# Router products and sums of squares computed as four 32-column strips of TensorE

## The chip, the cores and the metric

One core of a Trainium2 chip runs the whole kernel. The metric is device time of one execution in microseconds (us). The kernel before has a median of 809.95 us over three runs, which lie between 808.85 and 810.82 us. The profile is of one further execution, taken by the hardware profiler.

## The reference, cut to what matters

One decoder layer on 1024 tokens of width 1024, in float32: a norm with a modulation, two parallel branches (causal attention with 4 heads, and a recurrent branch of width 512), their projection added to the residual, then a router and 32 experts of which each token uses two.

```python
h = rms_norm(x, norm1_g) * (1.0 + scale1) + shift1
proj = h @ w_in
q_lat, kv_lat, k_rope, x_lru, g_lru = split(proj)
attn = mla_attention(q_lat, kv_lat, k_rope, ...)
lru = rg_lru_branch(x_lru, g_lru, ...)
mixed = concat([rms_norm(attn, attn_out_norm), rms_norm(lru, lru_out_norm)])
x = x + gate1 * (mixed @ w_out)
h2 = rms_norm(x, norm2_g) * (1.0 + scale2) + shift2

g_prob = softmax(t @ w_rg + b_rg)           # 4 groups; t is h2 as rows
e_logits = (t @ w_re + b_re)                # 32 experts, 8 in each group
# the best group, in it the two best experts, their weights g_p * e_p
# each expert on its tokens: (silu(xb @ w_gate[e]) * (xb @ w_up[e])) @ w_down[e]
x = x + gate2 * y
```

The change touches two things in it: the mean of the squares of `lru` over its 512 channels, for each token (inside the norm of the recurrent branch), and the 4 + 32 logits of each token.

## The kernel before, in words

The tokens are eight tiles of 128. The program goes through these stages: input projection with the recurrent branch (20 to 236 us of the profile), the projection of the recurrent branch by the lower half of `w_out` (`l_pass`, 236 to 300, merged with the preparation of the next attention heads), attention (to about 445), the projection of the attention output with the second norm, the router and the token tables (`w_steps`, mostly 445 to 515), and the experts (515 to the end), whose weights are streamed from HBM by SP in loads `ew` of 512 KB. Some of these loads are issued early, at points named by `ahead`, as far as buffers are free; at most four are in flight. SP works off its queue in order, so a store that waits holds back the weight loads behind it.

The order of instructions on each engine is not that of the code: a scheduler simulates the program as it is built and rewrites each engine's order. Any changed instruction can therefore move others. Banks of PSUM (matmul results) are handed out by tag from rings (`OPT["ph"]`): `pL` from a ring of three banks, `pr` from a ring of one, `pc2` from a ring of two that `ptq`, `ptk` and `ptk2` share.

The places that the change and the prediction touch:

- `norms` (L1055 to L1060) computes, for given tiles, the sum of squares over channels. `sqL` holds squares with channels on partitions and the 1024 tokens along the row, already added over the four channel blocks on POOL (L660). For each tile, L1059 loads 128 tokens of `sqL` as weights and multiplies by a column of ones: one column of output for each tile, with tokens on partitions. `rsq` (L197 to L213) turns it into the reciprocal root on DVE, in twelve small dependent steps, as `ivL`.
- `l_pass` (from L1062) needs `ivL` when it evicts the first product `pL` (DVE, L1082); a product is twelve matmuls of 512 columns (L225 to L227, three for each f32 product, on parts split into high and low).
- `x1_t` (L1250) transposes one token tile of the new residual (`pth`, L1257) and copies it on ACT to two halves `x1T` (L1258).
- `router(g)` (L1260 to L1268) serves a pair of tiles: with 128 tokens as weights and the 40 columns of `wrg` (4 group logits, 4 fillers, 32 expert logits) as the moving operand it accumulates eight products for each tile in `pr`. Each f32 product shows as two records in the trace.
- `route(g)` (from L1273) scales the logits by `ivx` (the second norm) and adds the bias on DVE (L1278), then finds groups, experts and weights in a chain of some thirty small DVE steps that ends in `mb` (L1311) and `rec`.
- `places(g)` (from L1319) turns `mb` into positions in the token table: PE `ppos`, DVE `scr`, `slot`, `ohs`, `rhs` (L1331 to L1342), PE `ptab` (L1345), DVE `tb` (L1350). Its `macc` carries counts from pair to pair.
- `w_steps` calls these in turn for each pair while the next pair is projected; for the last pair the router stands behind the last projection, and the table, the gathers of tokens and the first expert follow from it. `h2_rows` scales a tile by `ivx` on ACT (L1242) and stores it through SP (L1247).

Of the kernel before, what the change touches and what calls it, by code (L numbers as in the profile page):

```python
# [20 lines left out]
D = 1024  # L21
S = 1024
NT = 8
# [77 lines left out]
for _n, _w in GRP:  # L101
# [20 lines left out]
def drain(g):  # L122
    for _ in g:
        pass
# [14 lines left out]
def layer(ctx, tc, A, out, dbg=None, stop=None):  # L139
# [57 lines left out]
    def rsq(o, ss, mul, eps, shape):  # L197
        x = smc.tile(shape, F32, name="rs_x")
        V.tensor_scalar(x, ss, mul, eps, op0=OP.mult, op1=OP.add)
        yield  # L200
        i = smc.tile(shape, I32, name="rs_i")
        V.tensor_scalar(i, x.bitcast(I32), 1, None, op0=OP.logical_shift_right)
        yield
        y = smc.tile(shape, F32, name="rs_y")
        V.tensor_scalar(y.bitcast(I32), i, -1, 0x5F3759DF, op0=OP.mult, op1=OP.add)
        yield
        t = smc.tile(shape, F32, name="rs_t")
        for it in range(3):
            V.tensor_mul(t, y, y)
            yield  # L210
            V.scalar_tensor_tensor(t, t, -0.5, x, op0=OP.mult, op1=OP.mult)
            yield
            V.scalar_tensor_tensor(o if it == 2 else y, t, 1.5, y, op0=OP.add, op1=OP.mult)  # L213
            yield
# [840 lines left out]
    def norms(iv, sq, ts):  # L1055
        n = len(ts)
        pc = bank("pc2")
        for t in ts:
            T.matmul(pc[:, t:t + 1], sq[:, t * 128:(t + 1) * 128], ones_c, start=True, stop=True)  # L1059
        drain(rsq(iv[:, ts[0]:ts[0] + n], pc[:, ts[0]:ts[0] + n], 1.0 / 512, EPS, [128, n]))  # L1060

    def l_pass():  # L1062
        mod_row("g1", 2)
# [196 lines left out]
    def router(g, parts=((0, 0), (0, 1), (1, 0), (1, 1))):  # L1260
        if "pr" not in St[g]:
            St[g]["pr"] = bank("pr")
        pr = St[g]["pr"]
        for a, h in parts:
            xT = St[2 * g + a]["x1T"]
            for k in range(4 * h, 4 * h + 4):
                T.matmul(pr[:, a * 40:a * 40 + 40], xT[h][:, (k % 4) * 128:(k % 4) * 128 + 128], wrg[:, k],
                         start=(k == 0), stop=(k == 7))  # L1268

    def two(w, name, dt=F32):  # L1270
        return sm.tile([128, 2, w], dt, name=name, bufs=2)

    def route(g):  # L1273
        pr = St[g].pop("pr")
        ts = slice(2 * g, 2 * g + 2)
        L = two(40, "L")
        for a in range(2):
            V.scalar_tensor_tensor(L[:, a], pr[:, a * 40:a * 40 + 40], ivx[:, 2 * g + a:2 * g + a + 1], brow,  # L1278
                                   op0=OP.mult, op1=OP.add)
        g8, gi, gex, gp = two(8, "g8"), two(8, "gi", U32), two(4, "gex"), two(1, "gp")  # L1280
        for a in range(2):
            V.max(g8[:, a], L[:, a, :8])
        ng = two(1, "ng")
        V.tensor_scalar(ng, g8[:, :, 0:1], -1.0, None, op0=OP.mult)
        for a in range(2):
            V.max_index(gi[:, a], g8[:, a], L[:, a, :8])
            SC.activation(gex[:, a], L[:, a, :4], AF.Exp, bias=ng[:, a], accum_out=gp[:, a])
        gf = two(1, "gf")
        V.tensor_copy(gf, gi[:, :, 0:1])
        oh = two(4, "oh")  # L1290
        V.tensor_tensor(oh, iota[:, None, :4].to_broadcast([128, 2, 4]), gf.to_broadcast([128, 2, 4]), op=OP.is_equal)
        sel = two(32, "sel").rearrange("p a (g e) -> p a g e", g=4)
        V.tensor_mul(sel, L[:, :, 8:].rearrange("p a (g e) -> p a g e", g=4), oh[:, :, :, None].to_broadcast([128, 2, 4, 8]))
        el = two(8, "el")
        V.tensor_reduce(el, sel.rearrange("p a g e -> p a e g"), op=OP.add, axis=AX.X)
        V.reciprocal(gp, gp)
        e8, ei = two(8, "e8"), two(8, "ei", U32)
        for a in range(2):
            V.max(e8[:, a], el[:, a])
        d = two(1, "d")  # L1300
        V.tensor_sub(d, e8[:, :, 1:2], e8[:, :, 0:1])
        SC.activation(d, d, AF.Exp)
        for a in range(2):
            V.max_index(ei[:, a], e8[:, a], el[:, a])
        ef = two(2, "ef")
        V.tensor_copy(ef, ei[:, :, 0:2])
        V.scalar_tensor_tensor(ef, gf.to_broadcast([128, 2, 2]), 8.0, ef, op0=OP.mult, op1=OP.add)
        V.tensor_tensor(M[:, ts], iota[:, None, None, :32].to_broadcast([128, 2, 2, 32]),
                        ef[:, :, :, None].to_broadcast([128, 2, 2, 32]), op=OP.is_equal)
        mb = sm.tile([128, 2, 32], BF, name="mb", bufs=2)  # L1310
        V.tensor_add(mb, M[:, ts, 0], M[:, ts, 1])  # L1311
        w1 = two(1, "w1")
        V.tensor_scalar(w1, d, 1.0, None, op0=OP.add)
        V.reciprocal(w1, w1)
        V.tensor_mul(rec[:, ts, 0, 1:2], w1, gp)
        V.tensor_mul(rec[:, ts, 1, 1:2], rec[:, ts, 0, 1:2], d)
        St[g]["mb"] = mb
# [38 lines left out]
    def w_steps():  # L1356
        for t in range(OPT["xa"]):
            load_x1(t)
        for g in range(4):
            while g not in fin:  # L1360
                yield False
            t = 2 * g
            load_x1(t + OPT["xa"])
            load_x1(t + 1 + OPT["xa"])
            drain(w_mm(t, 0))
            if g:
                x1_t(t - 1)
                router(g - 1)
                norm2([t - 2, t - 1])
            ahead(4 * g)  # L1370
            yield True
            drain(w_mm(t, 1))
            if g:
                route(g - 1)
            x1_t(t)
            ahead(4 * g + 1)
            yield True
            drain(w_mm(t + 1, 0))
            if 0 < g < 3:
                places(g - 1)  # L1380
            ahead(4 * g + 2)
            yield True
            drain(w_mm(t + 1, 1))
            if g:
                h2_rows(t - 2)
                h2_rows(t - 1)
            ahead(4 * g + 3)
            yield True
        mod_row("g2", 5)
        ahead(16)  # L1390
        norm2([6])
        x1_t(7, (0,))
        router(3, ((0, 0), (0, 1)))
        x1_t(7, (1,))
        router(3, ((1, 0), (1, 1)))
        places(2)
        norm2([7])
        route(3)
        h2_rows(6)
        h2_rows(7)  # L1400
        ahead(17)
        places(3)
# [372 lines left out]
```

## Time and profile before

| | |
|---|---|
| median of three runs | 809.95 us (808.85 to 810.82) |
| profiled execution | 816.49 us |
| its span, first to last instruction | 814.6 us |
| mean granted clock of TensorE | 0.971 |
| PE busy | 728.1 us, 89% of the span |
| PE weight loads busy | 471.2 us, 58% (beside PE) |
| DVE, ACT, POOL busy | 447.2 us (55%), 317.0 us (39%), 157.6 us (19%) |
| moved by DMA | 180.47 MB, 222 GB/s over the span |

The profiled execution took 1.9 us more than its span, and 6.5 us more than the median. A share of busy time is an average over stages with different limits: PE is the busy engine until about 500 us, the DMA engines are the busy ones behind it. A matmul's end in the trace is modelled, so what one costs is read from the distance of two starts, not from its length. The rows further down are read in that way.

### The profile page before, as it was taken

How to read it: one execution, taken by the hardware profiler on the slowest of the kernel's cores; microseconds unless marked ns; L12 is line 12 of the kernel's file. 1: busy time of each engine (PE TensorE's matmuls, PEld its weight loads, DVE VectorE, ACT ScalarE, POOL GpSimd, SP SyncE). 2: the span in 40 equal slices, each digit the busy share in tenths (PEclk: the TensorE clock that was granted, in tenths of full speed). 3: DMA queues.
4: the chain of work that ended last, by engine and by line, in shares of the span. 5: the costliest groups of instructions: out<-in, count | busy, mean ns of one | idle time of the engine just before them, and what ended most of it. 6: DMA issues, size and time to landing. Idle time of an engine off the chain costs nothing. (4 is left out here: it accounts for less than half of the span.)

```text
span 814.6 us, 12260 instructions
## 1 busy us (share of the span) xinstructions
PE 728.1 (89%) x4257; PEld 471.2 (58%) x4257; DVE 447.2 (55%) x1334; ACT 317.0 (39%) x715; POOL 157.6 (19%) x150
## 2 busy tenths in 40 slices
PE   3899999989988989899999997699979899999874
PEld 1477776548877878788888886333333343332321
DVE  4597386868777469797884667344334222213210
ACT  3455456666354157667664434121201211102200
POOL 1121012103665102031311000212112112212010
PEclk9989999999999999999999998699989999999998
DMA  9952437681317403020154789999999999999994
GB/s 311 372 151 84 143 108 236 210 280 58 109 44 259 168 39 104 1 79 1 54 173 144 259 311 343 346 316 349 313 373 330 329 335 336 369 347 354 304 320 102
DMA packets 70976, 180.47 MB, mean 222 GB/s; under 512 B 8960, under 2 KB 22528, under 8 KB 70912
## 3 DMA queue, kind: packets, MB, share of 16 engines
q1 hardware_dynamic: 63328, 158.50, 55.1%
q0 software_dynamic: 7104, 21.00, 9.5%
q8 instruction: 34, 0.56, 0.3%
q10 hardware_dynamic: 480, 0.16, 0.2%
q14 instruction: 30, 0.25, 0.1%
HBM read 160.61 MB, written 22.95 MB: 225 GB/s over the span
## 5 line engine op out<-in xcount | busy, mean ns | idle before, releaser
L1649 PE MATMUL pgu<-ew,xeT 128*32 128x512 f32 (+1 forms) x928 | 163.4, 613 | 8.1 <-DMA ew<-in_w_e 7.3
L1649 PEld LDWEIGHTS pgu<-ew,xeT 128*32 128x32 f32 (+1 forms) x928 | 48.3, 121 | 99.4 <-issue 79.0
L1660 PE MATMUL py<-ew,hT 128*32 128x512 f32 (+1 forms) x464 | 75.1, 597 | 5.8 <-ACT hT L1634 5.8
L225 PE MATMUL pp<-hTh,winh 128*128 128x512 f32 x176 | 69.2, 406 | 5.8 <-DVE hTh L188 3.0
L226 PE MATMUL pp<-hTl,winh 128*128 128x512 f32 x176 | 71.1, 404 | 0.0
L227 PE MATMUL pp<-hTh,winl 128*128 128x512 f32 x176 | 70.4, 401 | 0.0
L1663 DVE TENSOR_TENSOR y<-py,m_g 128x512 f32<-128x512 f32 (+1 forms) x40 | 27.5, 691 | 69.3 <-PE py L1660 64.3
L1623 ACT ACTIVATE sg<-pgu 128x256 f32<-128x256 f32 (+1 forms) x20 | 7.7, 387 | 142.9 <-PE pgu L1649 135.8
L1660 PEld LDWEIGHTS py<-ew,hT 128*32 128x32 f32 (+1 forms) x464 | 23.5, 120 | 48.3 <-issue 35.7
L1616 DVE TENSOR_SCALAR xeT<-pxe,gc,mc 128x128 f32<-128x128 f32 x80 | 27.4, 404 | 33.0 <-PE pxe L1610 33.0
L225 PEld LDWEIGHTS pp<-hTh,winh 128*128 128x128 f32 x176 | 34.0, 194 | 16.3 <-DVE hTh L188 4.0
L1665 POOL DMA_INDIRECT out<-y,pki x13 | 20.7, 1589 | 111.2 <-DVE y L1663 87.7
L1625 DVE SCALAR_TENSOR_TENSOR hid<-sg,pkw,pgu 128x256 f32<-128x256 f32 (+1 forms) x13 | 6.2, 479 | 63.4 <-ACT sg L1623 60.9
L1634 ACT ACTIVATE hT<-pht 128x256 f32<-128x256 f32 (+1 forms) x20 | 7.6, 380 | 85.1 <-PE pht L1632 65.4
L1614 ACT ACTIVATE xeT<-pxe,mc,gc 128x128 f32<-128x128 f32 x80 | 30.0, 461 | 24.9 <-PE pxe L1610 24.9
L226 PEld LDWEIGHTS pp<-hTl,winh 128*128 128x128 f32 x176 | 33.9, 193 | 9.9 <-issue 2.1
L227 PEld LDWEIGHTS pp<-hTh,winl 128*128 128x128 f32 x176 | 34.1, 194 | 8.6 <-issue 1.7
L949 ACT ACTIVATE P<-pS,nb,scq 128x384 f32<-128x384 f32 (+2 forms) x48 | 32.3, 679 | 12.2 <-DVE nb L946 12.2
L983 PE MATMUL po<-PT,v 128*128 128x256 f32 (+1 forms) x160 | 35.8, 362 | 0.0
L1046 POOL TENSOR_TENSOR wo<-wo,m_g 128x256 f32<-128x256 f32 x32 | 28.2, 916 | 15.3 <-DMA wo<-in_w_out 15.3
L983 PEld LDWEIGHTS po<-PT,v 128*128 128x128 f32 x160 | 28.8, 191 | 2.9
L1610 PEld LDWEIGHTS pxe<-ident,xe 128*128 128x128 f32 x160 | 18.2, 145 | 20.7 <-issue 14.4
(424 smaller groups left out, 1613.6 us busy)
## 6 DMA issues: line engine op xcount, KB each, us to landing
ew<-in_w_e SPq DMA_DIRECT2D x186, 512.0 KB
wad<-in_w_ada SPq DMA_DIRECT2D x64, 256.0 KB
wada<-in_w_ada SPq DMA_DIRECT2D x16, 512.0 KB
win<-in_w_in SPq DMA_DIRECT2D x12, 512.0 KB
xt<-in_x SPq DMA_DIRECT2D x8, 512.0 KB
wo<-in_w_out SPq DMA_DIRECT2D x8, 512.0 KB
xr<-in_x SPq DMA_DIRECT2D x8, 512.0 KB
x_d<-xr SPq DMA_DIRECT2D x8, 512.0 KB
```

The source lines that it names most:

```text
L225: T.matmul(o, lhi, rhi, start=first, stop=False)
L226: T.matmul(o, lhi, rlo, start=False, stop=False)
L227: T.matmul(o, llo, rhi, start=False, stop=last)
L949: SC.activation(Pt[:, o:o + w], pss[ci], AF.Exp, scale=P["scq"][:, i:i + 1], bias=nb, accum_out=l[:, ci:ci + 1])
L983: T.matmul(po[:, o:], P["v"][:, js], PT[j // 4][:, j % 4, o:], start=(j == 0), stop=(j == nj - 1), skip_group_check=True)
L1046: EN[OPT["g1"]].tensor_mul(w[:, q:q + 256], w[:, q:q + 256], mrow["g1"][:, q:q + 256])
L1614: SC.activation(xT[a][:, c], pt[:, c], AF.Identity, scale=gc[:, k:k + 1], bias=sh2[:, k:k + 1])
L1616: last["dve"] = V.tensor_scalar(xT[a][:, c], pt[:, c], gc[:, k:k + 1], sh2[:, k:k + 1], op0=OP.mult, op1=OP.add).ins
L1649: T.matmul(pg[r], xT[k // 4][:, c + r.start:c + r.stop], w[k // 2][:, NS[k % 2]], start=(k == 0), stop=(k == 7), skip_group_check=True)
L1660: T.matmul(py[n][r], hT[:, a * 128 + r.start:a * 128 + r.stop], w[4 + a][:, NS[n]], start=(a == 0), stop=(a == 1), skip_group_check=True)
L1663: last["dve"] = V.tensor_mul(y[:rows, NS[n]], py[n][:rows], mrow["g2"][:rows, NS[n]]).ins
L1665: G.indirect_dma_start(out=out, out_offset=bass.IndirectOffsetOnAxis(ap=idx, axis=0), in_=y[r0:r0 + idx.shape[0]], in_offset=None, compute ...
```

## The change

`norms` for all eight tiles (the one call for `sqL`) now makes 32 columns of ones the weights and lets the squares move: each of four matmuls takes 256 tokens and writes its sums to 32 partitions of its own of one bank, as a strip. ACT copies the bank to `sqr`, PE transposes its two halves to bring tokens back to partitions, DVE copies every 32nd column to `ivL`, and `rsq` works in place. The norms of the attention output keep the old path.

`router4(g)`, for the first three pairs, makes 32 columns of `wrg` the weights and lets 128 tokens move. A product of the two tiles is four strips: the 32 expert logits of each tile, and columns 0 to 31 of `wrg` of each tile, of which only the first eight are used. The 32 matmuls of a pair fill one bank of 128 x 128; ACT copies it to `rt`, PE transposes it into a bank of a new tag `prt`, and `route` reads the four parts with four instructions where it had two. The last pair keeps the old path.

```diff
--- before
+++ after
@@ -107,7 +107,7 @@
         {"tags": {"pp": "A", "pt": "C", "pg": "C", "pkv": "C", "pq": "C", "pm": "D", "pL": "A", "pc2": "E", "pm2": "E", "pmc": "E", "pc": "E",
                   "pk": "E", "ptq": "E", "ptk": "E", "ptk2": "E"}, "n": {"A": 3, "C": 2, "D": 1, "E": 2}},
         {"tags": {"pS": "A", "ptP": "A", "po": "D", "pkv": "E", "pq": "E", "ptq": "E", "ptk": "E", "ptk2": "E", "pc2": "E",
-                  "pth": "A", "pr": "D", "pA": "A", "ppos": "B", "pbr": "B", "ptab": "B"}, "n": {"A": 4, "D": 1, "E": 2, "B": 1}},
+                  "pth": "A", "pr": "D", "prt": "E", "pA": "A", "ppos": "B", "pbr": "B", "ptab": "B"}, "n": {"A": 4, "D": 1, "E": 2, "B": 1}},
         {"tags": {"pA": "A", "ptab": "D", "pth": "E", "pr": "C", "ppos": "B", "pbr": "B", "pc2": "B"},
          "n": {"A": 3, "D": 1, "E": 2, "C": 1, "B": 1}},
         {"tags": {"pgu": "A", "py": "B", "py1": "B", "pxe": "C", "pht": "E", "pcn": "E", "pP": "E", "pT": "E", "psort": "E",
@@ -1055,9 +1055,21 @@
     def norms(iv, sq, ts):
         n = len(ts)
         pc = bank("pc2")
-        for t in ts:
-            T.matmul(pc[:, t:t + 1], sq[:, t * 128:(t + 1) * 128], ones_c, start=True, stop=True)
-        drain(rsq(iv[:, ts[0]:ts[0] + n], pc[:, ts[0]:ts[0] + n], 1.0 / 512, EPS, [128, n]))
+        if n < NT:
+            for t in ts:
+                T.matmul(pc[:, t:t + 1], sq[:, t * 128:(t + 1) * 128], ones_c, start=True, stop=True)
+            drain(rsq(iv[:, ts[0]:ts[0] + n], pc[:, ts[0]:ts[0] + n], 1.0 / 512, EPS, [128, n]))
+            return
+        for j in range(4):
+            T.matmul(pc[32 * j:32 * j + 32, :256], ones_f[:, :32], sq[:, j * 256:(j + 1) * 256], start=True, stop=True,
+                     skip_group_check=True)
+        sr = half("sqr")[:, :256]
+        SC.activation(sr, pc[:, :256], AF.Copy)
+        pt = bank("pc2")
+        for j in range(2):
+            T.transpose(pt[:, j * 128:(j + 1) * 128], sr[:, j * 128:(j + 1) * 128], ident)
+        V.tensor_copy(iv.rearrange("p (s h) -> p h s", h=2), pt[:, 0:256:32].rearrange("p (h s) -> p h s", h=2))
+        drain(rsq(iv, iv, 1.0 / 512, EPS, [128, n]))
 
     def l_pass():
         mod_row("g1", 2)
@@ -1267,14 +1279,32 @@
                 T.matmul(pr[:, a * 40:a * 40 + 40], xT[h][:, (k % 4) * 128:(k % 4) * 128 + 128], wrg[:, k],
                          start=(k == 0), stop=(k == 7))
 
+    def router4(g):
+        pr = bank("pr")[:, :128]
+        for k in range(8):
+            for j in range(4):
+                xT = St[2 * g + j % 2]["x1T"]
+                c = 8 if j < 2 else 0
+                T.matmul(pr[32 * j:32 * j + 32], wrg[:, k, c:c + 32], xT[k // 4][:, (k % 4) * 128:(k % 4) * 128 + 128],
+                         start=(k == 0), stop=(k == 7), skip_group_check=True)
+        rt = half("rt")[:, :128]
+        SC.activation(rt, pr, AF.Copy)
+        St[g]["pt"] = bank("prt")
+        T.transpose(St[g]["pt"][:, :128], rt, ident)
+
     def two(w, name, dt=F32):
         return sm.tile([128, 2, w], dt, name=name, bufs=2)
 
     def route(g):
-        pr = St[g].pop("pr")
         ts = slice(2 * g, 2 * g + 2)
         L = two(40, "L")
-        for a in range(2):
+        for a in range(2) if "pt" in St[g] else ():
+            pr = St[g]["pt"]
+            for o, c, w in ((8, 32 * a, 32), (0, 64 + 32 * a, 8)):
+                V.scalar_tensor_tensor(L[:, a, o:o + w], pr[:, c:c + w], ivx[:, 2 * g + a:2 * g + a + 1], brow[:, o:o + w],
+                                       op0=OP.mult, op1=OP.add)
+        for a in range(2) if "pr" in St[g] else ():
+            pr = St[g]["pr"]
             V.scalar_tensor_tensor(L[:, a], pr[:, a * 40:a * 40 + 40], ivx[:, 2 * g + a:2 * g + a + 1], brow,
                                    op0=OP.mult, op1=OP.add)
         g8, gi, gex, gp = two(8, "g8"), two(8, "gi", U32), two(4, "gex"), two(1, "gp")
@@ -1365,7 +1395,7 @@
             drain(w_mm(t, 0))
             if g:
                 x1_t(t - 1)
-                router(g - 1)
+                router4(g - 1)
                 norm2([t - 2, t - 1])
             ahead(4 * g)
             yield True
```

What stands in the order of instructions at three places, before and after. Line numbers of the two differ by 12 from `norms` on and by 30 from `route` on.

PE, the router of the second pair (`pr_4781` before, `pr_4805` after), first before:

```order
1824 L1257 MATMUL pth_4768<-ident_134,xr2_4348 128x128 [waits DMAHW3_49,Activation_49]
...
1826 L1267 MATMUL pr_4781<-wrg_4042,x1T_4667 128x40
...
1829 L1267 MATMUL pr_4781<-wrg_4042,x1T_4667 128x40 x3
1830 L1267 MATMUL pr_4781<-wrg_4042,x1T_4674 128x40 x4
...
1848 L1267 MATMUL pr_4781<-wrg_4042,x1T_4767 128x40 [waits Activation_49]
1849 L1267 MATMUL pr_4781<-wrg_4042,x1T_4767 128x40 x3
1850 L1267 MATMUL pr_4781<-wrg_4042,x1T_4774 128x40 [waits Activation_49]
1851 L1267 MATMUL pr_4781<-wrg_4042,x1T_4774 128x40 x3
1852 L1257 MATMUL pth_4883<-ident_134,xr2_4350 128x128 [waits DVE_49]
```

and after:

```order
1873 L1375 MATMUL ptab_4731<-rhs_4732,ohs_4734 128x64 [waits DVE_49,PE_49]
...
1876 L1288 MATMUL pr_4805<-x1T_4791,wrg_4044 32x128 [waits Activation_49]
1877 L1288 MATMUL pr_4805<-x1T_4691,wrg_4044 32x128
...
1891 L1288 MATMUL pr_4805<-x1T_4698,wrg_4044 32x128
1892 L225 MATMUL pA_4935<-woh_2306,mAh_4398 128x512
...
1896 L226 MATMUL pA_4935<-wol_2331,mAh_4398 128x512
1897 L1288 MATMUL pr_4805<-x1T_4798,wrg_4044 32x128 [waits Activation_49]
1898 L1288 MATMUL pr_4805<-x1T_4698,wrg_4044 32x128
...
1911 L1288 MATMUL pr_4805<-x1T_4798,wrg_4044 32x128
1912 L227 MATMUL pA_4935<-woh_2330,mAl_4399 128x512
...
1930 L227 MATMUL pA_4975<-woh_2388,mAl_4399 128x512
1931 L1293 MATMUL prt_4840<-ident_134,rt_4838 128x128 [waits Activation_49]
1932 L225 MATMUL pA_5007<-woh_2306,mAh_4502 128x512 [waits Activation_49]
```

The 32 products stood in four places between transposes. Now they stand in two runs of 16 and 15 (rows 1876 to 1891 and 1897 to 1911), behind a single one further up, with five matmuls of `pA` between the runs, and the transpose `prt` follows nineteen `pA` matmuls later.

PE, the projection of the recurrent branch; before, from the end of its second product on:

```order
865 L227 MATMUL pL_2096<-woh_2022,mLl_2056 128x512
866 L851 MATMUL ptq_2110<-ident_134,qnp_1990 128x128 [waits DVE_49,PE_49]
...
877 L227 MATMUL pL_2122<-woh_2022,mLl_2056 128x512
878 L863 MATMUL ptk_2136<-ident_134,kraw_1702 128x128 [waits DVE_49]
...
880 L225 MATMUL pL_2143<-woh_1953,mLh_2055 128x512 [waits DVE_49]
...
891 L227 MATMUL pL_2143<-woh_2022,mLl_2056 128x512
892 L868 MATMUL ptk2_2157<-ident_134,sqh_1704 128x128 [waits DVE_49,PE_49]
...
894 L851 MATMUL ptq_2233<-ident_134,qnp_2086 128x128 [waits DVE_49]
...
897 L851 MATMUL ptq_2363<-ident_134,qnp_2204 128x128 [waits DVE_49]
...
900 L225 MATMUL pL_2185<-woh_1953,mLh_2173 128x512 [waits Activation_49]
```

and after:

```order
843 L1064 MATMUL pc2_2030<-sqL_1613,ones_f_130 32x256 [waits Pool_49]
844 L1064 MATMUL pc2_2030<-sqL_1613,ones_f_130 32x256
845 L227 MATMUL pL_2069<-woh_1953,mLl_2058 128x512 [waits DVE_49]
...
865 L227 MATMUL pL_2098<-woh_2000,mLl_2058 128x512
866 L1070 MATMUL pc2_2037<-ident_134,sqr_2035 128x128 [waits Activation_49]
867 L1070 MATMUL pc2_2037<-ident_134,sqr_2035 128x128
868 L225 MATMUL pL_2098<-woh_2022,mLh_2057 128x512
...
871 L851 MATMUL ptq_2112<-ident_134,qnp_1990 128x128 [waits DVE_49]
...
880 L863 MATMUL ptk_2138<-ident_134,kraw_1702 128x128 [waits DVE_49]
...
882 L868 MATMUL ptk2_2159<-ident_134,sqh_1704 128x128 [waits DVE_49,PE_49]
...
884 L851 MATMUL ptq_2235<-ident_134,qnp_2088 128x128 [waits DVE_49]
...
887 L225 MATMUL pL_2145<-woh_1953,mLh_2057 128x512 [waits DVE_49]
```

The transposes of the sums (L1070) stand 21 matmuls of `pL` behind the last strip. Before the fourth product (`pL_2143`, now `pL_2145`) there now stand `ptk2` and a `ptq`, which came behind it. On ACT the copy `sqr` is put ahead of the six instructions that read the two `pq` banks.

DVE, the last two pairs; before:

```order
945 L1278 SCALAR_TENSOR_TENSOR L_5057<-pr_4991,ivx_1618,brow_4044 128x40 [waits PE_49]
946 L1278 SCALAR_TENSOR_TENSOR L_5057<-pr_4991,ivx_1618,brow_4044 128x40
...
955 L1233 SCALAR_TENSOR_TENSOR ivx_1618<-nv3_5162,nv2_5161 128x1 [waits DVE_49]
...
972 L1311 TENSOR_TENSOR mb_5094<-M_4046 128x64 [waits DVE_49]
...
974 L1214 SCALAR_TENSOR_TENSOR xr2_4749<-pA_5131,ivA_1616,xr2_4749 128x512 [waits PE_49]
...
978 L1331 TENSOR_TENSOR scr_5211<-ppos_5205,M_4046 128x128 [waits PE_49]
...
989 L1338 TENSOR_TENSOR rhs_5216<-M_4046,rec_4049 128x256 [waits DVE_49]
...
991 L1278 SCALAR_TENSOR_TENSOR L_5244<-pr_5181,ivx_1618,brow_4044 128x40 [waits PE_49]
...
997 L1278 SCALAR_TENSOR_TENSOR L_5244<-pr_5181,ivx_1618,brow_4044 128x40 [waits DVE_49]
```

and after:

```order
952 L1226 SCALAR_TENSOR_TENSOR xr2_4773<-pA_5199,ivA_1616,xr2_4773 128x512 [waits PE_49]
...
954 L1304 SCALAR_TENSOR_TENSOR L_5123<-prt_5072,ivx_1618,brow_4046 128x32 [waits PE_49]
955 L1304 SCALAR_TENSOR_TENSOR L_5123<-prt_5072,ivx_1618,brow_4046 128x8
956 L1304 SCALAR_TENSOR_TENSOR L_5123<-prt_5072,ivx_1618,brow_4046 128x32
957 L1304 SCALAR_TENSOR_TENSOR L_5123<-prt_5072,ivx_1618,brow_4046 128x8
...
962 L1245 SCALAR_TENSOR_TENSOR ivx_1618<-nv3_5230,nv2_5229 128x1 [waits DVE_49]
...
992 L1341 TENSOR_TENSOR mb_5162<-M_4048 128x64 [waits DVE_49]
...
994 L1308 SCALAR_TENSOR_TENSOR L_5312<-pr_5249,ivx_1618,brow_4046 128x40 [waits PE_49]
995 L1308 SCALAR_TENSOR_TENSOR L_5312<-pr_5249,ivx_1618,brow_4046 128x40
996 L1361 TENSOR_TENSOR scr_5279<-ppos_5273,M_4048 128x128 [waits PE_49]
...
1006 L1372 TENSOR_TENSOR ohs_5290<-iota_141,slot_4047 128x256
...
1008 L1368 TENSOR_TENSOR rhs_5284<-M_4048,rec_4051 128x256 [waits DVE_49]
```

The `ivx` row in the middle is that of the last tile but one. The logits of the third pair (`L_5057`, now `L_5123`) were read ahead of both halves of the last tile's `xr`; they are now read behind the second half, which waits for the last `pA`. So the chain of the third pair, up to its `mb`, stands whole between the end of the projection and the logits of the last pair (`L_5244`, now `L_5312`), and the `scr` to `rhs` of its places stand among the steps of the last pair's chain, where they stood ahead of it.

## Rows read from the trace of the kernel before

**Rows 1.** Busy time by stretch (busy us and instructions, clock, DMA share, GB/s)

```profile
244.00:300.00 56.00, 50.72 (x256) 41.83 (x255) 32.13 (x65) 19.35 (x43) 14.70 (x17) 1.00 0.45 169
...
515.00:814.00 299.00, 265.38 (x1634) 98.83 (x1632) 82.17 (x243) 44.45 (x121) 50.37 (x38) 0.96 0.94 320
```

**Rows 2.** Waits of SP's queue, 505 to 545 (us in total, times, longest)

```profile
SPq L1125 <- PE pgu L1649: 9.7, 6, 2.9
```

**Rows 3.** Timeline of PE, second pair's router (start us, length us)

```profile
465.85 1.65 PE L1267 MATMUL pr<-wrg,x1T 128*128 128x40 f32 x14
467.33 0.48 PE L225 MATMUL pA<-woh,mAh 128*128 128x512 f32 x1
```

**Rows 4.** Timeline of PE, four strips of `pm` side by side, near the start

```profile
28.09 1.50 PE L445 MATMUL pm<-wada,cs 128*32 128x256 f32 x24
...
35.10 0.40 PE L225 MATMUL pp<-hTh,winh 128*128 128x512 f32 x1
35.43 0.64 PE L445 MATMUL pm<-wada,cs 128*32 128x256 f32 x8
...
36.33 0.40 PE L227 MATMUL pp<-hTh,winl 128*128 128x512 f32 x1
```

**Rows 5.** Timeline of PE's weight loads, the same set of strips

```profile
35.42 0.16 PEld L445 LDWEIGHTS pm<-wada,cs 128*32 128x32 f32 x8 [0.37 <-issue]
```

**Rows 6.** Timeline of PE, sums of squares

```profile
235.21 1.14 PE L820 MATMUL pq<-wq,latq 128*128 128x192 f32 x6
236.19 0.95 PE L1059 MATMUL pc<-ones_f,sqL 128*128 128x1 f32 x8
237.00 0.49 PE L225 MATMUL pL<-woh,mLh 128*128 128x512 f32 x1
237.32 0.40 PE L226 MATMUL pL<-wol,mLh 128*128 128x512 f32 x1
237.56 0.40 PE L225 MATMUL pL<-woh,mLh 128*128 128x512 f32 x1
```

**Rows 7.** Timeline of PE, idle time in the projection of the recurrent branch

```profile
251.88 0.44 PE L851 MATMUL ptq<-ident,qnp 128*128 128x128 f32 x2 [0.98 <-DVE ks L870]
253.11 0.50 PE L225 MATMUL pL<-woh,mLh 128*128 128x512 f32 x1 [0.58 <-ACT mLh L218]
```

**Rows 8.** Timeline of DVE, the reciprocal root of the sums

```profile
240.42 0.15 DVE L199 TENSOR_SCALAR rs_x<-pc 128x8 f32<-128x8 f32 x1
...
243.10 0.17 DVE L213 SCALAR_TENSOR_TENSOR ivL<-rs_t,rs_y 128x8 f32<-128x8 f32 x1
243.37 0.75 DVE L1082 SCALAR_TENSOR_TENSOR xr<-pL,ivL,xr 128x512 f32<-128x512 f32 x1
```

**Rows 9.** Timeline of PE, from the last projection to the first expert

```profile
496.40 1.43 PE L1267 MATMUL pr<-wrg,x1T 128*128 128x40 f32 x12
...
505.50 0.18 PE L1325 MATMUL ppos<-mb,tri 128*128 128x32 bf16 x1 [3.36 <-DVE mb L1311]
...
520.53 1.17 PE L1649 MATMUL pgu<-ew,xeT 128*128 128x512 f32 x1
```

**Rows 10.** Timeline of DVE, the chains of the last two pairs

```profile
490.68 0.43 DVE L1278 SCALAR_TENSOR_TENSOR L<-pr,ivx,brow 128x40 f32<-128x40 f32 x2 [0.16 <-PE pr L1267]
...
495.13 0.22 DVE L1311 TENSOR_TENSOR mb<-M 128x64 bf16<-128x64 f32 x1
...
501.07 0.26 DVE L1278 SCALAR_TENSOR_TENSOR L<-pr,ivx,brow 128x40 f32<-128x40 f32 x1
...
505.23 0.22 DVE L1311 TENSOR_TENSOR mb<-M 128x64 bf16<-128x64 f32 x1
...
505.84 0.29 DVE L1331 TENSOR_TENSOR scr<-ppos,M 128x128 f32<-128x128 f32 x1 [0.31 <-PE ppos L1328]
...
507.24 0.42 DVE L1338 TENSOR_TENSOR rhs<-M,rec 128x256 f32<-128x256 f32 x1
```

**Rows 11.** Timeline of SP's queue, weight loads behind that tile's store

```profile
496.17 2.44 SPq L1125 DMA_DIRECT2D ew<-in_w_e  x3
```

## The prediction

> **What bounds the kernel now.** I read the busy time by stretch first. In the experts, from 515 us on, the DMA engines are busy for 0.94 of the time at 320 GB/s while PE has idle time [rows 1]: the end follows the stream of expert weights. That stream can be moved from in front only in one way. Behind 505 us SP, which issues it, waited 9.7 us in six pieces for buffers that the first experts' products still held [rows 2]. So a microsecond by which the first expert starts earlier or later (520.53 us [rows 9]) reaches the end almost whole, as long as the loads are there. In front of it PE has almost no idle time in the places that the change touches, except in the projection of the recurrent branch: 50.72 us busy of 56 between 244 and 300 us [rows 1]. Then comes a tail in which DVE decides: behind the last projected product, at 496.40 us (called T0 below), PE makes the last pair's router, and later waits 3.36 us for `mb`, the end of DVE's routing chain, before it can build the table [rows 9]. So I ask three things: what do the strips cost on PE, what does the later `ivL` do, and what does the new order do to DVE's chain behind T0.
>
> **Price of a strip.** The trace before has strips of the same kind, the 256-column f32 products `pm` at the start. Two more sets of four (24 records against 8) take 1.50 - 0.64 = 0.86 us, so 0.43 us for a set [rows 4]. One f32 product on the full array costs the same for each column: six records of 192 columns, three products, start 0.98 us before what follows, 1.70 ns a column, 0.44 us for 256 [rows 6]. So four strips go in the time of one, and the eight loads of a set lie within 0.16 us [rows 5]: the columns decide. A set of four with 128 columns, as in `router4`, is then 0.22 us. Going into strips and back is not free: from a 512-column product before a set to the second product behind it pass 36.33 - 35.10 = 1.23 us, of which the two such products alone need 0.48 (237.32 to 237.56 us [rows 6]) and the set 0.43; some 0.32 us are left for each run of strips [rows 4].
>
> The Trainium skill says, in "TensorEngine Tiling (Array Packing)", section Key Properties, that a change of tiling mode drains TensorE, and this trace agrees, with those 0.32 us. Its section Theoretical Speedup gives up to four times for a small dimension of at most 32. By that the three pairs' products would take a quarter of what they take; the rows give about a half, because the old form was never paid by its 40 columns.
>
> **Router, three pairs.** Before: 14 records in 467.33 - 465.85 = 1.48 us, 0.106 us each, 32 records for a pair, 3.38 us, 10.1 us for three [rows 3]. After, by the order: a pair has one strip alone (0.22 + 0.32 = 0.54 us) and, in the first pair, one run of 31 strips, in the others runs of 16 and 15. The first pair: 0.54 + 8 x 0.22 + 0.32, and one transpose at 0.11 (taken as one record of the old router) = 2.7 us, 0.7 less. The others: 0.54 + 4 x 0.22 + 0.32 + 4 x 0.22 + 0.32 + 0.11 = 3.05 us, 0.33 less. Together 1.35 us less. Bounds: with no price for the switch the three pairs cost 5.6 us, 4.5 less; if only two of four strips went side by side, a set would cost 0.44, the three pairs 5.3 more than I take, which is 4 us more than before. The rows stand with the first reading, and close to it. The copy of `pr` on ACT and the two more reads on DVE (some 0.2 us each, from 0.43 for two [rows 10]) lie beside PE's projection for the first two pairs.
>
> **Sums of squares.** Before: two groups of eight records, 237.00 - 236.19 = 0.81 us each [rows 6]. After: the strips come two and two, each group 0.43 + 0.32 = 0.75 us, and two transposes, 0.22: 0.1 us more. Bounds, as for the set: 0.5 less, 1 more. What hangs on it is larger. `ivL` was ready at 243.27 us [rows 8]. The last strips end at about 239.2 us, the transposes stand 21 products behind, 21 x 0.23 = 4.8 us, at 244.0; DVE's copy follows to 244.5, and the root takes its 2.85 us (240.42 to 243.27 [rows 8]): `ivL` at 247.4, four microseconds late, the first eviction (0.75 us [rows 8]) done at 248.2 to 248.4. All three banks of `pL` are full until then. PE has other work first, since `ptk2` and a `ptq` were put ahead of the fourth product: by 0.23 for each of nine products and 0.11 for each of eighteen transposes it comes there at 248.1. So it waits 0.1 to 0.5 us. In return it comes to the next pair of tiles early: 12 products more, at some 251.1 us, one `ptq` (0.44 us) still to do, where before two idle pieces of 0.98 and 0.58 us lay in front of 253.11 [rows 7]. That is 1.5 us of gain. What is late next: three evictions in a row on DVE, and `qnp` and the squares of `pq`, which on ACT now stand behind the copy of the sums, and must wait till 239.2. I take 1.1 us of gain, and keep 1.5 of gain and 2 of loss (half the delay of `ivL`) as ends.
>
> **The tail.** Before, the third pair's chain ran from 490.68 to `mb` at 495.13, ahead of T0, beside the last projection; the fourth's from 501.07 to 505.23, T0 + 8.83 [rows 10]. Now the third pair's logits are read behind the last eviction, which ends at T0 + 0.95 (0.75 [rows 8] and some 0.2 to start, an estimate from `ppos` at 505.50 and `scr` at 505.84 [rows 9, 10]). Its chain was 4.45 us with one eviction of 0.75 in it: 3.7, and 0.4 for two more reads: its `mb` at T0 + 5.2. The last pair's router is done by then (its logits were read at T0 + 4.67), so they follow at T0 + 5.4; its chain needs 3.7, as the third pair's, and between its steps stand `scr` to `rhs` of the third pair, 507.66 - 505.84 = 1.8 us [rows 10]: T0 + 10.9, 2.1 late. Part of these 1.8 fills gaps between dependent steps; I take 1.6 late, ends 0.5 and 2.1. And `ivx` of tile 6 now ends amid the first steps of that chain, so its rows are stored some 3.5 us behind T0 (an estimate: 2.2 to there, the rest for ACT and the issue), and that store stands in SP's queue ahead of three weight loads, issued until now from T0 - 0.2 on [rows 11]. Three loads are 1.5 MB, 4.8 us of the stream at 320 GB/s; SP's waits for buffers of 9.7 us [rows 2] cover most. I take 0.3 us late, ends 0 and 1.
>
> **Sum.** Router -1.35, sums +0.1, projection -1.1, tail +1.6, loads +0.3: -0.45 us. By the profile's own execution 816.49 becomes 816.0; that execution lies 6.5 us over the median, with the same stages, so I put the same difference on the median: 809.95 becomes 809.5. A measurement of this kernel tells 0.2%, 1.6 us, from no change.
>
> **Rivals.**
> - *The chain behind T0 takes more than PE gives back (slower).* Place: DVE, from the last eviction to the fourth `mb`. Price: 2.1 us late, and the loads 1 us, against 1.35 - 0.1 from the strips; the early start in the projection is lost again in the waits up to 300 us. Sum: 3.1 - 1.25 = 1.85, 811.8 us. It decides as soon as the projection gains less than 0.3 us. For it: PE already waits for `mb` for 3.36 us [rows 9], so nothing covers it. Against: DVE's steps can share gaps.
> - *Both PE stages give what they can (faster).* The switches at half their price: router -2.6, sums -0.2; projection -1.5, tail +0.5: -3.8 us, 806.1. For it: the idle pieces [rows 7] stand where PE would now work. Against: the price of the switch is read, not guessed.
> - *Strips go only two at a time (slower).* Router 5.3 and sums 0.9 above what the sum takes: 815.7. Against: 0.43 us for a set and 0.44 for one product [rows 4, 6].
> - *The products are a quarter (faster).* A quarter of 10.1 is 2.5 us, 7.6 less where I take 1.35 less: 803.2. Against: 32 strips with 128 columns each need 1.74 us a pair even with no switch. The Trainium skill's Theoretical Speedup, named above, is the rule for this.
> - *The weight stream hides it all (no change).* 809.95: with 0.94 of DMA busy [rows 1] the loads would have to arrive as before whatever PE does. Against: 9.7 us of waiting for buffers [rows 2].
>
> **Chances.** The forecast 0.33 and the hidden change 0.13, both within 0.2%: 0.46. The chain behind T0 0.21, strips two at a time 0.05: slower 0.26. Both stages in full 0.25, the quarter 0.03: faster 0.28. The likeliest case alone runs from 808.4 to 811.2. For 8 in 10 the range must take in both near rivals with their own spread, 805.9 to 813.2; outside lie the two far ones and the ends of the near ones.
>
> **What would show it.** Right: two runs of strips in PE's timeline of 1.2 us each in the second and third pair, 2.1 in the first; `ivL` near 247.4 us, followed by a wait of PE under 0.5 us at the fourth product; the 0.98 and 0.58 us gone; the last projected product about 2.3 us earlier; the fourth pair's `mb` 10.4 us behind it instead of 8.83; the first expert some 0.7 us earlier. Wrong: a run of 16 strips over 1.6 us (no full overlap); idle time of PE over 1 us at the fourth product; a fourth `mb` less than 9.3 or more than 11 us behind T0; or a first expert that moves while the end does not, which would be the stream.

## The result, and the profile after

The changed kernel takes 819.38 us, median of 11 runs (813.19 to 820.46), against 810.82 us (808.85 to 814.02, 11 runs) for the one before: a ratio of 1.0084, 95% interval 1.0059 to 1.0109, some 7 us slower. The forecast was 809.5 us, range 805.9 to 813.2.

The two profiled executions don't show this in their spans: 814.1 us after, 814.6 before. The part from the first expert's first product to the end took 286.4 us in the one and 294.1 in the other, and lay between 286.2 and 295.1 over the eleven profiles of this study, though none of the kernels changes anything there. So the stages in front of it are compared, between four marks in PE's timeline: the start of the sums of squares, an early wait of the attention, the start of the last product of the projection `pA` (within 0.3 us of T0), and the first expert's first product.

| us | sums to attention | attention to last `pA` | last `pA` to first expert | sums to first expert |
|---|---|---|---|---|
| before | 77.17 | 182.81 | 24.36 | 284.34 |
| after | 79.89 | 187.76 | 25.25 | 292.90 |
| difference | +2.7 | +5.0 | +0.9 | +8.6 |

The loss lies in front of the first expert, and 7.7 of its 8.6 us lie in two stages that were forecast to gain.

**The projection of the recurrent branch.** PE's timeline of after, from the second pair of strips on (start us, length us, engine, line, what, count, idle time in front in brackets):

```profile
236.94 0.63 PE L1064 MATMUL pc<-sqL,ones_f 128*32 128x256 f32 x4
...
249.37 0.63 PE L868 MATMUL ptk<-ident,sqh 128*128 128x128 f32 x4 [3.62 <-DVE rs_t L209]
250.49 0.46 PE L851 MATMUL ptq<-ident,qnp 128*128 128x128 f32 x2 [0.50 <-DVE kTl L222]
...
251.15 0.79 PE L225 MATMUL pL<-woh,mLh 128*128 128x512 f32 x1
251.74 0.63 PE L226 MATMUL pL<-wol,mLh 128*128 128x512 f32 x1
```

PE stands still for 3.62 us in front of `ptk2`, and the products behind it start 0.43 us apart where they started 0.23 apart [rows 6]. What PE waits for is not `ivL` itself but a bank. By the order in which the two banks of the ring are handed out, `ptk2` takes that of a `ptq`, whose last reader is `ql` on DVE; the `ptq` behind it waits in the same way for `kTl`, the last reader of `ptk`. On DVE `ql` stands among the steps of the root of `ivL` (and of a second root, `scq`, made beside it), and `kTl` right behind them, so both come as late as the root lets them. In DVE's timeline:

```profile
243.02 0.26 DVE L199 TENSOR_SCALAR rs_x<-ivL 128x8 f32<-128x8 f32 x1
...
244.71 0.74 DVE L209 TENSOR_TENSOR rs_t<-rs_y 128x8 f32<-128x8 f32 x2
...
248.82 0.41 DVE L857 TENSOR_TENSOR ql<-ptq,qs 64x256 fp32r<-64x256 f32 x1
249.15 0.22 DVE L209 TENSOR_TENSOR rs_t<-rs_y 128x8 f32<-128x8 f32 x2
...
249.53 0.17 DVE L213 SCALAR_TENSOR_TENSOR ivL<-rs_t,rs_y 128x8 f32<-128x8 f32 x1
```

`ql` ends at 249.23 us, just ahead of `ptk2`. The root starts at 243.02 and ends at 249.70: 6.7 us where it took 2.85 [rows 8]. Most pairs of steps on 128 x 8 numbers take 0.73 or 0.74 us together, until POOL's work beside them ends at 248.79; the first pair behind it takes 0.22. In POOL's and in SP's timeline:

```profile
236.94 11.85 POOL L1046 TENSOR_TENSOR wo<-wo,m_g 128x256 f32<-128x256 f32 x16
```

```profile
222.27 1.76 SPq L1040 DMA_DIRECT2D wo<-in_w_out  x4
251.78 0.33 SPq L1098 DMA_DIRECT2D x_d<-xr  x1
```

POOL scales the other half of `w_out` beside the root. It can, because its four loads now stand in SP's queue ahead of the first store of `x1_d`. Before, the first of them stood behind the first store, and three behind the second; SP's timeline of before:

```profile
251.26 1.75 SPq L1040 DMA_DIRECT2D wo<-in_w_out  x3
```

Why the scheduler moved them is not shown.

**The router stage.** PE's timeline of after, the first pair's run of strips, then the second pair:

```profile
454.43 1.95 PE L1288 MATMUL pr<-x1T,wrg 128*32 128x128 f32 x62
456.31 0.66 PE L1269 MATMUL pth<-ident,xr 128*128 128x128 f32 x4
...
469.74 0.18 PE L1355 MATMUL ppos<-mb,tri 128*128 128x32 bf16 x1
...
470.31 0.66 PE L1269 MATMUL pth<-ident,xr 128*128 128x128 f32 x4 [0.29 <-DVE xr L1226]
472.12 1.47 PE L1375 MATMUL ptab<-rhs,ohs 128*128 128x64 f32 x8 [1.16 <-DVE nv L1233]
473.51 1.94 PE L1288 MATMUL pr<-x1T,wrg 128*32 128x128 f32 x32
475.38 0.80 PE L225 MATMUL pA<-woh,mAh 128*128 128x512 f32 x1
...
476.71 0.40 PE L226 MATMUL pA<-wol,mAh 128*128 128x512 f32 x1
477.03 1.07 PE L1288 MATMUL pr<-x1T,wrg 128*32 128x128 f32 x30
478.04 0.50 PE L227 MATMUL pA<-woh,mAl 128*128 128x512 f32 x1
478.38 0.39 PE L225 MATMUL pA<-woh,mAh 128*128 128x512 f32 x1
```

The first run of 31 strips takes 1.88 us from its start to the start of what follows. In the second pair `ptab` stands directly ahead of the strips and waits 1.16 us. It waits for `rhs`, which DVE ends at 471.98 us (the bracket names a neighbour of `rhs` on DVE):

```profile
471.56 0.42 DVE L1368 TENSOR_TENSOR rhs<-M,rec 128x256 f32<-128x256 f32 x1
```

Before, six microseconds of PE's work lay between the start of `ppos` and this `ptab`; PE's timeline of before:

```profile
464.63 0.19 PE L1325 MATMUL ppos<-mb,tri 128*128 128x32 bf16 x1
...
470.61 1.00 PE L1345 MATMUL ptab<-rhs,ohs 128*128 128x64 f32 x8
```

The run of 16 behind `ptab` takes 1.87 us, the run of 15 at the end 1.01. In the busy time by stretch the granted clock (the column behind the five engines) falls to its lower level, 1.2 of 2.4 GHz, just there. It does so in the projection behind the 3.62 us as well, the first line here:

```profile
251.00:252.00 1.00, 1.00 (x4) 0.75 (x3) 1.00 (x3) 0.52 (x2) 0.00 (x0) 0.50 0.00 0
...
471.00:472.00 1.00, 0.00 (x0) 0.00 (x0) 1.00 (x4) 0.00 (x0) 0.08 (x1) 1.00 0.37 152
472.00:473.00 1.00, 0.88 (x7) 0.91 (x7) 0.83 (x6) 0.00 (x0) 0.00 (x0) 0.82 0.89 373
473.00:474.00 1.00, 1.00 (x15) 0.85 (x18) 0.39 (x4) 0.00 (x0) 0.00 (x0) 0.50 0.00 0
...
475.00:476.00 1.00, 1.00 (x14) 0.53 (x3) 0.09 (x1) 0.88 (x1) 0.00 (x0) 0.50 0.00 0
476.00:477.00 1.00, 1.00 (x5) 0.58 (x3) 0.00 (x0) 1.00 (x2) 0.00 (x0) 0.97 0.06 16
```

The third pair repeats this 20 us later, with the same 0.29 and 1.16 us. The tail then has the shape that was forecast; PE's timeline:

```profile
502.79 0.98 PE L1279 MATMUL pr<-wrg,x1T 128*128 128x40 f32 x8
...
513.34 0.18 PE L1355 MATMUL ppos<-mb,tri 128*128 128x32 bf16 x1 [0.52 <-DVE mb L1341]
...
527.70 4.70 PE L1679 MATMUL pgu<-ew,xeT 128*128 128x512 f32 x7
```

### The profile page after: what moved, and what is told of

Its sections match the earlier page's. It is cut to its first block, busy times and chain, and to the rows that moved or that the text cites. A ratio compares the mean times of both kernels' runs of the same rounds, so it can differ in the third digit from the quotient of the medians.

```text
span 814.1 us, 12451 instructions
## 1 busy us (share of the span) xinstructions
PE 728.5 (89%) x4350; PEld 466.8 (57%) x4350; DVE 451.4 (55%) x1341; ACT 318.1 (39%) x719; POOL 155.6 (19%) x150
## 5 line engine op out<-in xcount | busy, mean ns | idle before, releaser
L941 DVE TENSOR_REDUCE mx<-pS 128x1 f32<-128x384 f32 (+2 forms) x48 | 26.9, 560 | 3.8 <-PE pS L940 2.6
```

The lines of the kernel that those rows point to most:

```text
L941: V.tensor_reduce(mx[:, ci:ci + 1], p, op=OP.max, axis=AX.X)
```

## The experiments

All were timed in five rounds beside the kernel before on the same chip; a ratio stands with its 95% interval.

**norms_only**: the call in `w_steps` is the old one.

```diff
-                router4(g - 1)
+                router(g - 1)
```

> The sums of squares as strips, the router as before. Theory A (POOL's scaling of the moved wo loads runs beside the root of ivL and slows DVE, PE waits 3.6 us for ptk2 and falls to the lower clock): entry of the strips to the attention stage 2.7 us longer than before, router stage and tail as before, time 2 to 3.5 us above before. Theory B (the projection costs nothing, all of the loss is in the router stage): within 1 us of before.

1.0041 (1.0011 to 1.0071), 3.3 us. Sums to attention 79.85 us, +2.7; the router stage as before, 182.80. PE's timeline:

```profile
249.90 0.63 PE L868 MATMUL ptk<-ident,sqh 128*128 128x128 f32 x4 [3.70 <-DVE rs_t L209]
```

The loss of the projection stage belongs to this part alone. Theory B, by which it costs nothing, is out: by the stage, since the interval of the time alone reaches down to 0.9 us.

**norms_wo_held**: the same, with an edge from the stores to the loads.

```diff
+            i = SY.dma_start(w, A["w_out"][f * 128:(f + 1) * 128, :]).ins
+            if f < 4:
+                tc.add_manual_dep(i, stores[min(f, 1)].name, mybir.DependencyInfo(mybir.DependencyClass.NoSync, mybir.DependencyReason.DATA), reason="order")
```

> As norms_only, but the four wo loads are put behind the stores of x1_d again, as before. Theory A: the steps of the root take 0.24 us a pair again instead of 0.73, ivL comes some 3 us earlier than in norms_only, PE waits under 1 us at ptk2, time between 1.5 us below and 0.5 above before. Rival (the way strips, copy, transposes, copy is by itself what makes ivL late): the idle time of over 3 us at ptk2 stays, time 2 us or more above before.

1.0060 (1.0031 to 1.0089): no better than norms_only, so the expected time was wrong. The rival had the time right, but not the place. DVE's and PE's timelines, and POOL's:

```profile
244.62 0.24 DVE L209 TENSOR_TENSOR rs_t<-rs_y 128x8 f32<-128x8 f32 x2
...
246.96 0.17 DVE L213 SCALAR_TENSOR_TENSOR ivL<-rs_t,rs_y 128x8 f32<-128x8 f32 x1
```

```profile
246.80 0.63 PE L868 MATMUL ptk<-ident,sqh 128*128 128x128 f32 x4
...
266.12 0.50 PE L225 MATMUL pL<-woh,mLh 128*128 128x512 f32 x1 [2.60 <-DVE xr L1098]
```

```profile
254.08 15.57 POOL L1050 TENSOR_TENSOR wo<-wo,m_g 128x256 f32<-128x256 f32 x15 [16.19 <-DMA wo<-in_w_out]
```

The root is fast again, two steps in 0.24 us, and `ivL` is ready at 247.13, 11.4 us behind the start of the sums instead of 14.9. At this `ptk2` PE no longer waits. But `ivL` is still 4.3 us later than before (7.1 us behind the sums), and with it the evictions, the stores and the loads held behind them: the first is issued at 250.00 us, before at 245.55. So POOL scales late, and the splits of these weights (`wol`), which stand in DVE's order ahead of the evictions of `pL`, wait for it: PE loses 2.60 us there (before, 1.02 at a like place). At the next `ptk2` it waits another 1.56 us, for `kTl`. The strips cost the projection one way or the other; sums to attention 80.25 us, +3.1.

**loads_early**: no strips at all, only the loads moved as the change moved them.

```diff
-            if g == 1:
-                next(ow)
...
+                if t == 1:
+                    next(ow)
+                    SY.dma_start(x1_d[:128, :], x0)
+                x0 = x
...
+                if t:
+                    SY.dma_start(x1_d[t * 128:(t + 1) * 128, :], x)
```

> No strips at all: the kernel before, with the four wo loads put ahead of the stores of x1_d, as the change did. Theory (POOL's scaling beside DVE's root slows the root): two steps of the root take 0.6 to 0.75 us instead of 0.24, ivL comes 2.5 to 4 us later after the sums than before; the stage 0 to 2 us longer, since before the third product PE has other work. Rival (the steps are slow for another reason, such as the strips' path): 0.24 us as before.

1.0057 (1.0028 to 1.0085). DVE's and PE's timelines:

```profile
243.44 0.73 DVE L209 TENSOR_TENSOR rs_t<-rs_y 128x8 f32<-128x8 f32 x2
...
249.00 0.65 DVE L213 SCALAR_TENSOR_TENSOR ivL<-rs_t,rs_y 128x8 f32<-128x8 f32 x1
```

```profile
250.57 0.79 PE L225 MATMUL pL<-woh,mLh 128*128 128x512 f32 x1 [4.04 <-DVE xr L1096]
```

The root is slow without a strip in the stage: POOL beside it is enough. `ivL` comes 14.2 us behind the start of the sums instead of 7.1, which is 7.1 later where I expected 2.5 to 4. PE waits 4.04 us for the first eviction, and the stage is 4.0 us longer (sums to attention 81.18 us), not 0 to 2.

**router_only**: in `norms` the old path for every call (`if n <= NT:`).

> The router as strips for three pairs, the sums as before. Theory A (late prt, hence late positions, hence ptab in front of the strips waits 1.16 us in two pairs, and PE runs at the lower clock behind it): end of the last projection some 5 us later than before, first expert 5.8 us later, time 4.5 to 7 us above before; with norms_only it adds up to the whole. Rival (the parts disturb each other): clearly less than 4 us above before.

1.0083 (1.0049 to 1.0117), 6.7 us; attention to last `pA` 187.78, +5.0, with the same waits of 0.29 and 1.16 us; first expert 6.0 us later. As theory A had it. With norms_only's 1.8 us the delays of the first expert make 7.8 of the whole change's 8.6 us.

**router_filled**: as router_only, with work for PE in the wait.

```diff
-        ptab = bank("ptab")[:, :64]
+        pb = bank("ptab")
+        if g < 2:
+            for _ in range(6):
+                T.matmul(pb[:, 128:256], ident, ident, start=True, stop=True)
+        ptab = pb[:, :64]
```

> As router_only, with six products of the identity (128 columns each, some 1.3 us in all) in front of ptab of the first two pairs, in a part of ptab's bank that nobody reads; the order is otherwise that of router_only. Theory (PE waits 1.16 us for rhs there, and what follows runs at the lower clock because PE stood idle): the wait is still there as time, but the clock stays at 1.0, ptab and the run of 16 strips take 0.85 and 1.2 us again instead of 1.0 to 1.4 and 1.87, the last projection ends 2 to 3 us earlier than in router_only, time 2 to 3 us below router_only, 3.5 to 5 above before. Rival (the clock falls with the strips, not with the idle time): 0.5 in the same places, time as router_only.

1.0060 (1.0033 to 1.0087), by the ratios 1.9 us less than router_only, which the two intervals don't tell apart. The stage shows it: the last `pA` comes 3.2 us earlier than in router_only (184.56 us behind the attention's mark). PE's timeline:

```profile
467.30 1.50 PE L1368 MATMUL ptab<-ident 128*128 128x128 f32 x12
468.63 1.00 PE L1379 MATMUL ptab<-rhs,ohs 128*128 128x64 f32 x8
469.57 1.08 PE L1288 MATMUL pr<-x1T,wrg 128*32 128x128 f32 x32
470.58 0.50 PE L225 MATMUL pA<-woh,mAh 128*128 128x512 f32 x1
```

In its busy time by stretch, the microsecond of these strips:

```profile
470.00:471.00 1.00, 1.00 (x26) 0.76 (x19) 0.82 (x6) 0.00 (x0) 0.00 (x0) 1.00 0.06 16
```

`ptab` takes 0.94 us where it took 1.39 in after, the run of 16 strips 1.01 where it took 1.87, and the granted clock stays at 1.00 through both pairs. So the clock fell with the idle time, not with the strips, and gave 1.6 us of the loss of each of the two pairs (half of the 3.2); the rest is the wait.

**router_prt_first**: as router_only, but the transpose of the logits must stand ahead of the next tile's projection.

```diff
+            k = len(nc.cur_bb.bb.instructions)
...
+            if t % 2 == 1 and n == 0 and f == 0 and t > 1 and "prt" in St[t // 2 - 1]:
+                for i in nc.cur_bb.bb.instructions[k:]:
+                    if i.engine == T.engine:
+                        tc.add_manual_dep(i, St[t // 2 - 1]["prt"].name, mybir.DependencyInfo(mybir.DependencyClass.NoSync, mybir.DependencyReason.DATA), reason="order")
+                        break
```

> As router_only, but the transpose prt must stand ahead of the next tile's projection, so it follows its strips by one set of four transposes, and the positions of a pair stand 20 matmuls ahead of its ptab. The products are the same. Theory A (the order is what costs): no idle time at ptab, granted clock 1.0 through the stage, the strips' gain of about 1.2 us shows at the last projection, third pair's chain again ahead of it: time 0.5 to 2 us below before. Rival (strips themselves cost, by their switches or by the clock that falls with them): time 3 us or more above before and lower clock without idle time in front.

0.9978 (0.9953 to 1.0003), 1.8 us below before; the interval just takes in no change, but lies clear of router_only's. Attention to last `pA` 181.32 us, 1.5 less than before; no wait at `ptab`; the granted clock 1.00 from 450 to 495 us; and the tail as in before. The 31 strips stand in one run in every pair. PE's timeline, third pair and tail:

```profile
486.42 1.95 PE L1294 MATMUL pr<-x1T,wrg 128*32 128x128 f32 x62
...
488.86 0.33 PE L1299 MATMUL prt<-ident,rt 128*128 128x128 f32 x1
...
503.62 0.18 PE L1361 MATMUL ppos<-mb,tri 128*128 128x32 bf16 x1 [3.36 <-DVE mb L1347]
```

The same products, in another order, gain in the stage what the price of strips promised. The loss of the router stage was the order.

**router_no_lone** and **no_lone_again**: as router_prt_first, with the second tile's strips first.

```diff
-            for j in range(4):
+            for j in (1, 3, 0, 2):
```

> As router_prt_first, with the four strips of a product in another order (second tile first), so that no single strip can start before the second tile is there. Theory (each way into strips and back costs some 0.3 us): the single strip's 0.34 us of each pair goes, its place in the run costs 0.05, last projection 0.8 to 1 us earlier than in router_prt_first, time 2 to 4 us below before. Rival (the first expert is not what the end follows, or the lone strip hid in a wait): time as router_prt_first.

> router_no_lone once more, beside the same runs of before, for a second interval: 2 to 4 us below before if its first one holds, within 1 us if that was chance.

0.9960 (0.9931 to 0.9989) and 0.9967 (0.9935 to 0.9999): 808.0 and 808.6 us beside 811.9 and 812.1. This is the version that beats both kernels. Attention to last `pA` 180.40 and 180.38 us, 0.9 less than router_prt_first. PE's timeline, second pair:

```profile
466.89 1.96 PE L1294 MATMUL pr<-x1T,wrg 128*32 128x128 f32 x64
468.77 0.66 PE L1275 MATMUL pth<-ident,xr 128*128 128x128 f32 x4
470.50 0.33 PE L1299 MATMUL prt<-ident,rt 128*128 128x128 f32 x1 [1.08 <-ACT rt L1297]
```

32 strips in one run take 1.88 us, as 31 did; the single one had cost its 0.34 for nothing. The 1.08 us in front of `prt` (0.89 in router_prt_first) show that this order still loses something.

**both_ordered**: router_no_lone with the sums as strips.

> The whole change, with the router stage ordered as in router_no_lone. Theory (the two parts add up): entry to attention 2.7 us longer than before as in norms_only, last projection's stage 2.4 us shorter, time within 1.5 us of before. Rival (the parts help each other, the early entry of one hiding the other's wait): 2 us or more below before.

0.9992 (0.9961 to 1.0022). Sums to attention 79.92 us, attention to last `pA` 180.35: what one part gains the other loses. The parts add up, within the interval.

## Why the prediction was wrong, point by point

- **What bounds the kernel.** Right: the first expert's start reaches the end. Over the changed kernel and the nine of the experiments its shift against before goes from -2.7 to +8.6 us, that of the time (the ratio of each, times 811 us) from -3.2 to +6.8, and the two agree within 2 us, where the half width of an interval is some 2 to 3.
- **Price of a strip.** Right, in mechanism and nearly in size. Read as in [rows 4], from the product before a run to the second product behind it, the run of 15 takes 478.38 - 476.71 = 1.67 us, less 0.48 for two products 1.19, where I had 1.20. From start to start a run is shorter (15 strips 1.01 us, 31 or 32 strips 1.88, the single one 0.34, 449.85 to 450.19), since part of the switch falls on the neighbours. My sign of strips that don't fully overlap, a run of 16 over 1.6 us, came (1.87), but for another reason: the clock, since the same run takes 1.01 in router_filled.
- **Router, three pairs: the failed step.** I took "32 records for a pair" against runs of strips and nothing else, -1.35 us, with the rest of the stage as it was. My own rows of the order showed `ptab` directly ahead of the strips. I didn't ask what it waits for there. The chain is: `prt` stands nineteen products behind its strips, so the logits, `mb` and `ppos` come later, between `ppos` and its `ptab` there now stands one set of transposes, where there stood twelve products and more, so DVE's `slot` to `rhs` no longer lie beside products. (When this program runs, `mb` itself is in time: in the first pair it ends at 466.77 us, 3 us ahead of `ppos`. It is the place of `ppos` in the order that comes late.) That the order costs it is shown by router_prt_first; that 1.6 us of a pair are the clock, by router_filled. In the stage: twice 1.45 us of waiting and 1.6 of clock, less the 1.35 that I had forecast as gain, is 4.75, against 5.0 measured. So the term for the products held; the waits and the clock were missing from the sum.
- **Sums of squares: the second failed step.** "The root takes its 2.85 us" was taken over from before. It took 6.7, because SP's queue had changed and POOL worked beside it. I also counted `ptk2` and a `ptq` as work that PE does meanwhile, and put the wait behind them, at the fourth product; they waited themselves, for banks that DVE reads among and behind the root's steps. So the bound of 2 us of loss was too small, and PE's wait of "0.1 to 0.5" became 3.62 and 0.50 with 1.5 us of lower clock (seven products from 251.15 to 254.26 us, 3.1 us instead of 1.6). Of the time, 2.6 us came back, in idle pieces of before that are gone: 0.98 and 0.58 [rows 7], which I had counted, and 1.02 us at 263.52. The moved loads were in the order of SP; I had not listed them in the sum. With the root at its old speed, in norms_wo_held, `ivL` comes 11.4 us behind the start of the sums, where I had 11.2 (247.4 less 236.19). The stage still lost 3.1 us there, since the loads held behind the stores come later with `ivL`, a path that the sum lacked too.
- **Tail.** Right for the chain: `ppos` of the last pair 10.66 us behind the end of the last product instead of 9.10 [rows 9], 1.56 late where I had 1.6. The three weight loads are issued 3.7 us behind T0, as forecast; what they cost is not told apart from the spread of the expert stage. The first expert is only 0.9 late by this stretch, where tail and loads together were 1.9 in the sum, since the gather behind the chain waited less (1.22 us in front of the first tokens' transposes, 1.96 before).
- **Rivals.** The slower rival named a real delay, the third pair's chain behind T0, but not the one that decided. Strips going two at a time, and products for a quarter, are both refuted by the 1.88 us.

## What to carry to other kernels

When a scheduler reorders, price the neighbours, not only the instructions that are edited: for each moved group read what stands directly ahead of it and what that waits for, on PE, and follow every moved DMA to the engine that its arrival sets to work. A chain that hid beside a stream of products becomes a wait as soon as its consumer follows its producer closely. Pinning one transpose turned 6.7 us of loss into a time no longer than before (1.8 us less, with an interval from 3.8 less to 0.2 more), with the same arithmetic.

## What the runs showed of the hardware that I had not expected

- DVE's small steps slow down beside POOL: 0.73 to 0.74 us for two steps on 128 x 8 numbers with POOL multiplying 128 x 256 blocks, in three kernels (after, norms_only, loads_early), 0.24 without, in before and norms_wo_held. The step `qTl`, which reads a bank of PSUM, kept its 0.41 us beside POOL (246.75 us in after). The Trainium skill, "SBUF — State Buffer", section SBUF: two separate sides, says that the two share a pair of ports that one instruction holds to its end. The trace agrees: the two steps together take as long as one of POOL's products (11.85 us for sixteen, 0.74 each).
- A wait of PE of 0.29 us and then one of 1.16 us were followed by 3 to 4 us at half the clock, in both pairs. In before, 0.98 and then 0.58 us [rows 7] were not: the granted clock stayed at 1.00 from 250 to 256 us, and is 1.00 over the whole stage [rows 1]. Why the one and not the other is open.
- The same expert code took 286.2 to 295.1 us in different executions, a spread wider than any difference in time tried here. What makes it is open.
